# A decoder trunk on one core: the bias table's roundings, GpSimd's queue and the ninth weight chunk planned anew

## The chip, the core and the metric

The kernel runs on one core of one Trainium2 chip. A core has five engines that run beside each other, each with its own queue of instructions in a fixed order: TensorE (PE, matmuls; its weight loads are PEld), VectorE (DVE), ScalarE (ACT), GpSimd (POOL) and SyncE (SP, which here only issues transfers). Transfers between HBM and the on-chip memory run on 16 DMA engines. The metric is the device time of one execution in microseconds; lower is better. Times are compared by the median of several runs.

## What is computed

A trunk of two layers over x of 256 tokens by 1024 columns, all in float32. Layer 0 mixes tokens with a gated spatial unit, layer 1 with attention that has a relative-position bias; each layer then has a gated feed-forward part with a causal convolution of width 3. Each sub-layer ends in `x <- LayerNorm(alpha * x + f(x))`. Cut to what matters here:

```python
def conv_ffn(x, w_up, conv_w, conv_b, w_down):
    S = x.shape[1]
    h = x @ w_up                                   # (256, 1024) @ (1024, 5632)
    hp = jnp.pad(h, ((0, 0), (CONV_WIDTH - 1, 0), (0, 0)))
    hc = conv_b
    for j in range(CONV_WIDTH):
        hc = hc + conv_w[j] * hp[:, j:j + S]
    g, val = jnp.split(hc, 2, axis=-1)
    return (jax.nn.gelu(g) * val) @ w_down         # (256, 2816) @ (2816, 1024)

# in the attention: a table of 32 buckets by 16 heads, looked up by distance
s_own = s_own + bias_hb[:, rel_bucket(d_own)][None].astype(jnp.float32)
```

## The kernel before

**Two parts for each number.** TensorE multiplies in a rounded float32 format. So every weight and every activation is split into a high part (the number rounded) and a low part (what the rounding lost), and a product is three matmuls: high by high, high by low, low by high. `split` does that: ScalarE writes the rounded high part (`act`, line 381), VectorE subtracts it from the number (`tt`, line 387).

**Weights in chunks.** `stream` lists the weights in the order of their use in chunks of 128 partitions by 2048 columns, 1 MB each: among others 22 of `f_up0` (layer 0's up projection), 11 of `f_dn0` (its down projection), and the same for layer 1 (`f_up1`, `f_dn1`). A chunk of `f_dn` holds two k-steps, 128 rows of the weight each; chunk c holds k = 2c and 2c + 1. A chunk is loaded into a `raw` tile by SyncE (`load`), and `prep` has its parts written to a slot of `whi` and one of `wlo`; there are five such slots, so `spent(name, c)`, called when a chunk was used, prepares the chunk five places later. Two `raw` tiles take turns (some chunks have tiles of their own), so a load waits until the tile's last readers are done.

**Two ways to the low part.** Usually VectorE subtracts. For the chunks in `NEGATED` (from `ADDED`) and in `SIDE`, `lows` does it without VectorE's subtraction: ScalarE writes the negative of the high part into `wlo`, and a transfer that GpSimd issues reads the chunk from HBM a second time and adds it there. `ADDED` names chunk 13 of both `f_up` and chunks 1, 3 and 8 of both `f_dn`; `SIDE` is the second half of chunks 4, 5, 6 (`f_dn0`) or 5, 6, 7 (`f_dn1`). Chunks in `WHOLE`, `NEGATED` among them, are handled as one piece of 2048 columns, others in two halves of 1024. In `f_dn1` the last three chunks are in `SUMMED` too, and so in `WHOLE`: `with_sums` makes, on ScalarE, copies of some of their columns in `xt` with a row sum beside them, for the last LayerNorm.

**The down projection.** `project_out` runs over k = 0 to 15 for both token tiles t; then the last six k-steps (`TAIL`, chunks 8, 9 and 10) run for one token tile after the other, piece by piece of 512 columns. The chunks of `SEVEN` (4, 5, 6 or 5, 6, 7) are not multiplied step by step but in seven products of sums and differences (`seven`); `weight_sums` (VectorE and ScalarE) and `token_sums` (additions on GpSimd, line 634) make their operands, and `into_rest` adds their results to x on ScalarE and VectorE. `close` is the last LayerNorm.

**The bias table.** `build_bias` is called between the feed-forward part's up and down projection of layer 0. VectorE clears a buffer, four small transfers fill it, `parts` (two VectorE operations, lines 758 and 760) rounds it and writes the lost part of the table's rows, one matmul (line 772) makes the table of 16 heads by 384 distances, VectorE copies it out (line 774), and a transfer stores it (`rbscr`) for the attention, which reads it eight times.

**The order.** Nothing runs as it is recorded. `plan.op` records each operation with its engine, an estimated duration, and what it reads and writes. `Plan.emit` first gives each operation a due time, counted back from TensorE's line of matmuls; an operation's own `early` makes it due sooner. Then it plays the whole kernel through with one clock for each engine: the engine that can start first takes, of the operations that are ready, the one due first. TensorE's main matmuls keep their recorded order; those marked as fill (the table's matmul, transposes, scores) are put in when they are ready. The start times of this play give each engine's order; an operation with `after` is held until that one has been issued. On the chip each engine then runs its queue in that order, and waits at its head where an operand isn't there. In this play GpSimd's compute operations are engine "pool" and its adding transfers a separate engine "gq", with a model of a shared bus; on the chip both are one queue. `parts` is recorded as a TensorE fill of 645 ns.

## Time and profile before

| what | us |
|---|---|
| median of 3 runs | 559.65 |
| the three runs | 557.83 to 560.56 |
| the profiled execution | 558.85 |
| its span, first to last instruction | 557.1 |
| TensorE busy in it | 548.8 |
| VectorE busy | 479.1 |
| ScalarE busy | 396.5 |
| GpSimd busy | 51.7 |

A row of the timeline has start, length, engine, line, operation, the tiles written and read, shapes and a count; in brackets stands how long the engine was idle before it, and what ended the idle time. Starts are from the span's begin. The line of a helper (369, 381, 387, 391, 405) stands for many operations, so rows are told apart by tile, shape and time. Ends of matmuls are modelled: the distance from one start to the next says more than the length.

```profile
L381 ACT ACTIVATE whi<-raw 128x1024 fp32r<-128x1024 f32 (+2 forms) x150 | 175.4, 1203 | 43.4 <-DMA raw<-in_f_up 18.2
L387 DVE TENSOR_TENSOR wlo<-raw,whi 128x1024 fp32r<-128x1024 f32 (+2 forms) x138 | 186.1, 1370 | 18.1 <-ACT whi L381 16.5
...
wlo<-in_f_dn POOLq DMA_DIRECT2D x6, 1024.0 KB, 9.1
...
wlo<-in_f_dn POOLq DMA_DIRECT2D x6, 512.0 KB, 7.2
wlo<-in_f_up POOLq DMA_DIRECT2D x2, 1024.0 KB, 11.0
```

The first two rows are groups of instructions: count, busy time in all, mean length in ns, idle time before them. The others are transfers by what they write and read: count, size, and the median time from issue to landing. The six of 1 MB into `wlo` from `f_dn` are chunks 1, 3 and 8 of the two layers.

### The profile page before, as it was taken

The page shows a single profiled execution, that of the slowest core. Times are in us where ns is not written, and L with a number is a line of the kernel's source. Part 1 is how long each engine was busy: PE and PEld are TensorE (multiplying, and loading weights), DVE is VectorE, ACT ScalarE, POOL GpSimd, SP SyncE. Part 2 cuts the span into 40 slices and gives each one's busy share as a digit, 9 for nine tenths or more (in the row PEclk, how much of TensorE's full clock was granted, in tenths as well). Part 3 has the DMA queues.
Part 4 walks back from the last instruction along what each step waited for, and adds up shares of the span by engine and source line. Part 5 has one row for each costly group of instructions (what it writes and reads, how often), then busy time and mean ns, then how long its engine had stood idle before and what let it go on. Part 6 is the DMA issues. An engine that isn't in the chain of part 4 may idle for free.

```text
span 557.1 us, 8253 instructions
## 1 busy us (share of the span) xinstructions
PE 548.8 (99%) x3024; PEld 471.0 (85%) x3024; DVE 479.1 (86%) x860; ACT 396.5 (71%) x669; POOL 51.7 (9%) x60
## 2 busy tenths in 40 slices
PE   9999999999999999999999999999999999999995
PEld 6889888988898887888888888788888888888884
DVE  6699989999989888898957778798969889997687
ACT  6647576688878786845567868577747969897951
POOL 0011110000003521001000000000000000053101
PEclk9999999999999999999999999999999999999998
DMA  8979624645954799893656252725754956799832
GB/s 325 390 284 355 222 99 161 260 184 228 240 213 166 232 283 301 219 356 115 235 218 194 103 191 86 296 77 191 263 188 191 259 203 235 282 268 321 185 100 77
DMA packets 22610, 122.51 MB, mean 220 GB/s; under 512 B 2519, under 2 KB 5801, under 8 KB 10409
## 3 DMA queue, kind: packets, MB, share of 16 engines
q1 hardware_dynamic: 19240, 110.18, 53.4%
q0 software_dynamic: 3040, 11.54, 11.3%
q8 instruction: 24, 0.39, 0.3%
q10 hardware_dynamic: 288, 0.26, 0.1%
q14 instruction: 18, 0.14, 0.1%
HBM read 120.90 MB, written 1.07 MB: 219 GB/s over the span
## 4 chain that ended last, share of the span: by engine, by line
PE 63%; DVE 14%; DMA 12%; ACT 7%; issue 3%; DVEq 0%; SPq 0%; ACTq 0%
PE bank L369 40%; PE twos L369 22%; DVE wlo L387 5%; DMA raw<-in_f_up 5%; DMA raw<-in_f_dn 4%; DVE ff L391 3%; ACT whi L381 3%; DVE ff L387 2%; DMA ff<-in_f_dn 2%; DMA wlo<-in_f_dn 2%; ACT wlo L381 1%; ACT ff L381 1%; DVE x L391 1%; PE twos L375 1%; DVE rr L387 1%
## 5 line engine op out<-in xcount | busy, mean ns | idle before, releaser
L381 ACT ACTIVATE whi<-raw 128x1024 fp32r<-128x1024 f32 (+2 forms) x150 | 175.4, 1203 | 43.4 <-DMA raw<-in_f_up 18.2
L387 DVE TENSOR_TENSOR wlo<-raw,whi 128x1024 fp32r<-128x1024 f32 (+2 forms) x138 | 186.1, 1370 | 18.1 <-ACT whi L381 16.5
L369 PE MATMUL bank<-xt,whi 128*128 128x512 f32 x512 | 121.2, 391 | 0.0
L369 PE MATMUL bank<-whi,rr 128*128 128x512 f32 x354 | 112.5, 391 | 0.0
L369 PEld LDWEIGHTS bank<-xt,whi 128*128 128x128 f32 x512 | 94.7, 188 | 18.7
L369 PEld LDWEIGHTS bank<-whi,rr 128*128 128x128 f32 x354 | 66.5, 188 | 14.0 <-issue 0.3
L369 PE MATMUL twos<-xt,whi 128*128 128x512 f32 x326 | 76.3, 390 | 0.0
L369 PEld LDWEIGHTS twos<-xt,whi 128*128 128x128 f32 x326 | 60.6, 188 | 12.2
L391 DVE SCALAR_TENSOR_TENSOR ff<-ff,convc 128x255 f32<-128x255 f32 (+1 forms) x160 | 69.4, 488 | 0.5
L369 PE MATMUL bank<-wlo,rr 128*128 128x512 f32 x177 | 69.1, 390 | 0.0
L369 PEld LDWEIGHTS bank<-xt,wlo 128*128 128x128 f32 x512 | 64.2, 191 | 2.0 <-issue 0.3
L369 PE MATMUL bank<-xt,wlo 128*128 128x256 f32 x512 | 65.6, 284 | 0.0
L381 ACT ACTIVATE ff<-ff,convc 128x256 f32<-128x256 f32 x80 | 44.5, 593 | 12.2 <-DVE ff L387 12.1
L369 PE MATMUL twos<-whi,xt 128*128 128x512 f32 x128 | 42.1, 396 | 0.0
L369 PE MATMUL twos<-xt,wlo 128*128 128x256 f32 (+1 forms) x323 | 41.2, 284 | 0.0
L369 PEld LDWEIGHTS twos<-xt,wlo 128*128 128x128 f32 x323 | 40.3, 191 | 1.0
L369 PEld LDWEIGHTS bank<-wlo,rr 128*128 128x128 f32 x177 | 33.2, 188 | 6.9 <-DMA wlo<-in_f_dn 0.3
L381 ACT ACTIVATE ff<-bank 128x256 f32<-128x256 f32 (+2 forms) x62 | 23.2, 393 | 17.4 <-PE bank L369 16.4
L381 ACT ACTIVATE ff<-bank,lncol 128x128 f32<-128x128 f32 x48 | 18.9, 458 | 21.0 <-PE bank L375 21.0
L369 PEld LDWEIGHTS twos<-whi,xt 128*128 128x128 f32 x128 | 24.1, 188 | 4.7
L634 POOL TENSOR_TENSOR lnrow<-lnrow 128x128 f32<-128x128 f32 x24 | 22.6, 1130 | 45.5 <-ACT ff L381 37.5
L381 ACT ACTIVATE ff<-twos 128x512 f32<-128x512 f32 (+1 forms) x36 | 18.6, 549 | 9.2 <-PE twos L369 5.7
(158 smaller groups left out, 689.9 us busy)
## 6 DMA issues: line engine op xcount, KB each, us to landing
raw<-in_f_up SPq DMA_DIRECT2D x44, 1024.0 KB, 4.8
raw<-in_f_dn SPq DMA_DIRECT2D x20, 1024.0 KB, 6.3
raw<-in_b_qk SPq DMA_DIRECT2D x8, 1024.0 KB, 4.8
wlo<-in_f_dn POOLq DMA_DIRECT2D x6, 1024.0 KB, 9.1
lnrow<-in_lnrow SPq DMA_DIRECT2D x5, 1024.0 KB, 6.8
raw<-in_a_out SPq DMA_DIRECT2D x4, 1024.0 KB, 7.5
raw<-in_b_v SPq DMA_DIRECT2D x4, 1024.0 KB, 5.0
raw<-in_b_o SPq DMA_DIRECT2D x4, 1024.0 KB, 4.8
```

The lines of the kernel that those rows point to most:

```text
L369: nc.tensor.matmul(o, l, x, start=start, stop=stop)
L375: nc.tensor.transpose(o, x, ident.ap)
L381: return plan.op("act", ns, lambda: nc.scalar.activation(o, x, func, **kw), r, w, table=table)
L387: return dve(70 + 1.04 * flat(x), lambda: nc.vector.tensor_tensor(o, x, y, op=op), r, w)
L391: lambda: nc.vector.scalar_tensor_tensor(o, x, s, y, op0=op0, op1=op1), r, w)
L634: plan.op("pool", 1200, lambda: nc.gpsimd.tensor_tensor(o, x, y, op=op), r, w)
```

## The change

Three things, in the program alone; no product is changed.

- The ninth chunk (c = 8) of `f_dn0` and `f_dn1` leaves `ADDED`: its low part comes from VectorE's subtraction. In `f_dn1` it stays in `WHOLE`; in `f_dn0` it leaves that too and is split in two halves.
- In the plan, "gq" is gone: an adding transfer is an operation of "pool" that carries bytes. It holds GpSimd for 1200 ns, its landing is counted on a queue of all adding transfers at 170 bytes per ns with 2500 ns on top, and its own duration for the due times is 3700 + 3.0 ns per column instead of 3600 + 1.8.
- `parts` is recorded as an operation of VectorE of 500 ns that reads `raw` and writes a buffer of its own, which the table's matmul (170 ns) reads. The copy of the table's row is due 10 us sooner (`early`), and the matmul is held behind the step k = 5 of the second token tile, not k = 3.

```diff
-ADDED = {"f_up0": {13: "act"}, "f_up1": {13: "act"}, "f_dn0": {1: "act", 3: "act", 8: "act"}, "f_dn1": {1: "act", 3: "act", 8: "act"}}
+ADDED = {"f_up0": {13: "act"}, "f_up1": {13: "act"}, "f_dn0": {1: "act", 3: "act"}, "f_dn1": {1: "act", 3: "act"}}
...
-    LATE = {"pe": 200.0, "act": 140.0, "dve": 130.0, "pool": 200.0, "sp": 910.0, "gq": 910.0}
+    LATE = {"pe": 200.0, "act": 140.0, "dve": 130.0, "pool": 200.0, "sp": 910.0}
...
-        engines = ("pe", "act", "dve", "pool", "sp", "gq")
+        engines = ("pe", "act", "dve", "pool", "sp")
...
-        bus, table = 0.0, None
+        bus, added, table = 0.0, 0.0, None
...
-            if e == "gq":
+            if e == "pool" and o.nbytes:
                 bus = max(bus, s + 1100.0) + o.nbytes / 360.0
                 free[e] = s + 1200.0
-                o.end = max(bus + 1000.0, s + 2000.0 + o.nbytes / 200.0)
+                added = max(added, s + 1200.0) + o.nbytes / 170.0
+                o.end = added + 2500.0
...
     def lag(self, d, o):
+        if d.eng == "pool" and d.nbytes:
+            return 910.0
         if d.eng == o.eng:
-            return 0.0 if d.eng == "pe" else 910.0 if d.eng in ("sp", "gq") else 130.0
+            return 0.0 if d.eng == "pe" else 910.0 if d.eng == "sp" else 130.0
...
-        plan.op("gq", 3600 + 1.8 * flat(lv), lambda: nc.gpsimd.dma_start(
+        plan.op("pool", 3700 + 3.0 * flat(lv), lambda: nc.gpsimd.dma_start(
...
         b = half()
-        plan.op("pe", 645, parts, [raw], [b], True)
-        state["table"] = plan.op("pe", 1, lambda: nc.tensor.matmul(
-            b.ap[:HEADS, :DIST], cast[:two, :HEADS], cast[:two, HEADS:], start=True, stop=True), [raw], [b], True)
-        dve(400, lambda: nc.vector.tensor_copy(row.ap[:HEADS], b.ap[:HEADS, :DIST]), [b], [row])
+        c = Buf(cast)
+        dve(500, parts, [raw], [c])
+        state["table"] = plan.op("pe", 170, lambda: nc.tensor.matmul(
+            b.ap[:HEADS, :DIST], cast[:two, :HEADS], cast[:two, HEADS:], start=True, stop=True), [c], [b], True)
+        dve(400, lambda: nc.vector.tensor_copy(row.ap[:HEADS], b.ap[:HEADS, :DIST]), [b], [row]).early = 2 * SOON
...
-            if name == "f_dn0" and (k, t) == (3, NT - 1):
+            if name == "f_dn0" and (k, t) == (5, NT - 1):
                 state["table"].after = groups[-1]
```

## The prediction

> **What bounds the kernel now.** I read the page first (busy time, the row of slices, the chain), then who waited for whom, then the stretches that the change touches.

> ```profile
> span 557.1 us, 8253 instructions
> PE 548.8 (99%) x3024; PEld 471.0 (85%) x3024; DVE 479.1 (86%) x860; ACT 396.5 (71%) x669; POOL 51.7 (9%) x60
> ...
> PE   9999999999999999999999999999999999999995
> ```
> ```profile
> PE twos L772 <- DVE cast L760: 0.5, 1, 0.5
> ```
> ```profile
> 200.00:212.00 12.00, 11.54 (x54) 9.34 (x53) 10.19 (x20) 9.98 (x14) 2.10 (x2) 1.00 1.02 299
> ...
> 224.00:237.00 13.00, 13.00 (x58) 10.51 (x58) 10.10 (x10) 10.94 (x10) 1.20 (x1) 1.00 0.82 228
> 520.00:537.00 17.00, 17.00 (x76) 14.05 (x75) 11.13 (x12) 14.32 (x28) 1.22 (x1) 1.00 0.75 199
> 537.00:548.00 11.00, 11.00 (x58) 9.44 (x58) 10.73 (x20) 2.55 (x3) 1.00 (x1) 1.00 0.09 28
> 548.00:557.00 9.00, 2.38 (x20) 2.18 (x19) 5.33 (x17) 1.90 (x6) 0.91 (x1) 0.77 0.25 84
> ```

> TensorE is busy in every slice but the last, and 8.3 us of the span are not its own: the head before the first weights, some 6.7 us behind its last matmul, and one hole of half a microsecond, the table's matmul on line 772. In the stretches (columns: length, then busy time of PE, PEld, DVE, ACT, POOL, then clock, DMA share and GB/s) TensorE fills each one that the change touches except 200 to 212. So neither VectorE nor the transfers bound the kernel; they matter only where something comes late for TensorE. The change alters none of the 3024 matmuls but the place of one. It can win what TensorE waits inside the body, and a little of the tail; it can lose whatever new wait it makes.

> **The change, step by step. (a) The table's roundings.** Before, the two roundings of `parts` are recorded as TensorE work but run on VectorE; the matmul that reads them stands behind the fourth step of `f_dn0`.

> ```profile
> 211.00 0.39 PE L369 MATMUL bank<-whi,rr 128*128 128x512 f32 x1
> 211.85 0.34 PE L772 MATMUL twos<-cast 97*16 97x384 f32 x1 [0.46 <-DVE cast L760]
> 212.02 0.40 PE L369 MATMUL bank<-whi,rr 128*128 128x512 f32 x1
> ```
> ```profile
> 211.13 0.36 DVE L758 CAST cast<-ff 97x400 fp32r<-97x400 f32 x1
> 211.53 0.17 DVE L760 TENSOR_TENSOR cast<-ff,cast 33x16 fp32r<-33x16 f32 x1
> ```
> ```profile
> 228.14 0.39 PE L369 MATMUL twos<-whi,rr 128*128 128x512 f32 x1
> 228.37 0.39 PE L369 MATMUL bank<-whi,rr 128*128 128x512 f32 x1
> 228.66 0.50 PE L369 MATMUL bank<-wlo,rr 128*128 128x512 f32 x1
> 228.99 0.40 PE L369 MATMUL bank<-whi,rr 128*128 128x512 f32 x1
> ```

> ```profile
> 203.89 2.29 DVE L387 TENSOR_TENSOR wlo<-raw,whi 128x2048 fp32r<-128x2048 f32 x1 [1.48 <-ACT whi L381]
> ```

> Wide matmuls follow each other every 0.23 us (228.14 to 228.37). From 211.00 to the table's matmul it is 0.85, so 0.62 us is lost. The roundings came last: 0.36 + 0.17 us, ended at 211.70. Now the matmul stands two k-steps later (k = 5 instead of 3). A k-step is two token tiles by two pieces by three matmuls, 12 x 0.227 = 2.7 us, so it comes at about 216.7 and the roundings have 5 us more. Its own 0.17 us (211.85 to 212.02) stays. The roundings now carry a due time of their own that is long past, so VectorE will take them as soon as the plan thinks the table landed. If the plan thinks so too early, VectorE's queue stands still in front of them; the chunk that TensorE wants next (k = 4, at about 211.5) had its low part done at 206.2 (203.89 + 2.29), so some 5 us of such a halt are covered. The copy of the table's row needs its bank back before the products open, four k-steps behind 212.02, at 222.9, some 5 us after its new place. Gain between -0.6 (a halt as long as the old hole, at the new place) and +0.62; I take **0.6**, since both neighbours show 5 us of room.

> **(b) One queue for GpSimd.**

> ```profile
> 219.32 1.07 ACT L381 ACTIVATE whi<-ff 128x1024 fp32r<-128x1024 f32 x1 [1.19 <-DMA ff<-in_f_dn]
> ```

> No instruction is added. What changes is the plan: an adding transfer now counts 9.8 us instead of 7.3 for a whole chunk (3700 + 3.0 x 2048 against 3600 + 1.8 x 2048) and 6.8 instead of 5.4 for a half, so ScalarE's negations and the loads under them become due 2.6 or 1.3 us sooner. ScalarE has 2 us free in 200 to 212 to take that. The one place where such a transfer is late now is 228.37 to 228.99: two steps of 0.29 and 0.33 instead of 0.23, 0.16 us in all. Its transfer could not be planned much sooner, as ScalarE had waited for its source chunk until 219.32. Bounds: a gain of 0.16 up to a loss of one VectorE subtraction, 2.4 us (rival 3); I take **0**, the side that the row is nearer to.

> **(c) The ninth chunk.** Before, ScalarE writes the high part, then its negative, and GpSimd's transfer adds the chunk from HBM. After, VectorE subtracts.

> ```profile
> 228.35 1.90 ACT L381 ACTIVATE wlo<-whi 128x2048 fp32r<-128x2048 f32 x1
> ```
> ```profile
> 230.69 1.20 POOL L495 DMA_DIRECT2D wlo<-in_f_dn  x1 [8.04 <-ACT wlo L381]
> ```
> ```profile
> DMA to landing us min/median/max: 12.2/12.2/12.2
> ```
> ```profile
> 243.07 0.40 PE L369 MATMUL bank<-wlo,rr 128*128 128x512 f32 x1
> ```
> ```profile
> 233.59 2.36 DVE L387 TENSOR_TENSOR wlo<-raw,whi 128x1024 fp32r<-128x1024 f32 x2
> ...
> 525.79 2.29 DVE L387 TENSOR_TENSOR wlo<-raw,whi 128x2048 fp32r<-128x2048 f32 x1 [1.11 <-ACT whi L381]
> ```

> Each layer loses a 1.90 us pass of ScalarE and a 1 MB transfer, and VectorE gains 2.36 us (in `f_dn0`, where the chunk now goes in halves) or 2.29 us (in `f_dn1`, whole). VectorE is idle 2.9 us in 224 to 237 and 5.9 us in 520 to 537, so both fit, the first barely. In `f_dn0` the added part landed at 242.9 (230.69 + 12.2), and the first matmul that reads it starts at 243.07: nothing is lost there, 0.2 us from being lost. So removing it gains 0 in layer 0. In layer 1 it lies on the chain that ended last:

> ```profile
> 523.26 8.38 DMA wlo<-in_f_dn
> 531.66 2.85 ACT xt L381 x11
> 534.52 0.49 ACT ff L381
> ...
> 535.03 0.69 DVE ff L387
> ...
> 550.87 0.34 DVE x L387
> ```
> ```profile
> 550.11 0.28 PE L369 MATMUL twos<-whi,rr 128*128 128x256 f32 x1
> ```

> The copies of the sums (`with_sums`) waited for the transfer, and behind them on ScalarE stood the first copy of `into_rest` (534.52), although the products that it reads were done when the last one began, at 532.98 (row in d). With pass and transfer gone that copy can come up to 1.5 us sooner, and VectorE's run from 535.03 on with it; VectorE is full from 537 to 548 (10.73 of 11). But the end moves by little: the last addition (550.87) needs TensorE's last matmul, started at 550.11 and done some 0.3 later. So 0.4 us at most, none at least; I take **0.3**.

> **(d) The raw tile.** The ninth chunk's tile was free when ScalarE had read it; now VectorE reads it too, and the eleventh chunk's load waits for that.

> ```profile
> 520.10 0.33 SPq L405 DMA_DIRECT2D raw<-in_f_dn  x1
> ```
> ```profile
> DMA to landing us min/median/max: 5.7/5.7/5.7
> ```
> ```profile
> 532.98 0.39 PE L369 MATMUL bank<-whi,rr 128*128 128x512 f32 x1
> ```

> If the subtraction ends at X, the load lands at X + 5.7, ScalarE's pass takes 1.9 and VectorE's 2.3, so the low part is there at X + 9.9. The last product ends at 533.7 (532.98 and two more matmuls), then five k-steps of one piece come; the eleventh chunk is the fifth, 4 x 0.68 later at 536.4, its low part at 536.6. So X may be as late as 526.7; the earliest is 520.1 + 2.3 = 522.4.

> ```profile
> 521.05 1.22 DVE L387 TENSOR_TENSOR rr<-ff,rr 128x1024 fp32r<-128x1024 f32 x1 [1.36 <-ACT rr L381]
> 523.99 0.69 DVE L387 TENSOR_TENSOR rr<-lnrow,rr 128x512 fp32r<-128x512 f32 x1 [1.71 <-ACT rr L381]
> ```

> VectorE stood idle for 1.36, 1.71 and 1.11 us in front of 521.05, 523.99 and 525.79, waiting for ScalarE each time, so I take X near 524 and a cost of **0**; behind the next subtraction it would be 3.7 us (rival 2). In `f_dn0` the same load has 4 us more room.

> **The sum:** 0.6 + 0 + 0.3 = 0.9 us. The profiled execution took 558.85 us (span 557.1 and 1.75 around it), so 557.95 after. The three runs shown have their median at 559.65, 0.8 above it; I forecast **558.7** for the median, -0.2%.

> **Rivals.** About 0.5%, 2.8 us, is what a measurement of this kernel can tell from no change; the three runs alone lie 2.7 us apart.

> *1. Nothing comes out.* The hole at 211 is refilled by a wait of like size, and the tail hangs on TensorE's last matmul. For it: TensorE is 99% busy and 550.11 to 550.87 leaves little. Against: the 5 us of room. Time 559.6.

> *2. Slower: the raw tile comes free late.* VectorE takes the ninth chunk's subtraction behind the tenth's (525.79 + 2.29 = 528.1), so X = 530.4, the low part comes at 540.3 instead of 536.6, and TensorE stands for 3.7 us; behind the roundings that follow as well, which the timeline shows to end at 530.4, it is X = 532.7 and 6.0 us. It decides from X = 526.7 on. For it: VectorE's order goes by due times that come from TensorE's line, and the tile's release is a step that only lengthens a load's wait. Against: the gaps before 525.8. Time 562.4 to 564.7, say 563.

> *3. GpSimd is held.*

> ```profile
> L634 POOL TENSOR_TENSOR lnrow<-lnrow x24: 450/763/3036, 176.3 to 513.4; 128x128 f32<-128x128 f32 x24
> ```
> ```profile
> 176.78 2.39 POOL L634 TENSOR_TENSOR lnrow<-lnrow 128x128 f32<-128x128 f32 x1
> ```
> ```profile
> 176.43 2.43 DVE L387 TENSOR_TENSOR wlo<-raw,whi 128x2048 fp32r<-128x2048 f32 x1 [0.32 <-issue]
> ```

> A GpSimd addition takes 0.45 us at best and 2.39 when it starts under a VectorE subtraction of 2.43. If the joint order now puts additions ahead of a transfer that TensorE waits for already (228.66), or beside a new subtraction, that transfer is late by up to 2.4 us: 558.7 + 2.4 = 561.1. Against: the last addition of `f_dn0` was done by 196.6, and in `f_dn1` they end at 514, before the ninth chunk is there. [...]

> *4. Faster than can be seen.* All waits that the change touches come to 0.62 + 0.16 + 0.4 = 1.2 us, so only a draw of the runs gets below 556.9.

> **How the numbers follow.** Forecast 0.65; rival 1 0.17; rival 2 0.10; rival 3 0.03; rival 4 0.05. Slower by over 0.5% holds rival 2 and a sliver of the rest, 0.11; faster 0.05; within 0.5% 0.84. The range takes in the forecast with the spread of the runs (about 1.5 us either way), rival 1 and rival 3: 557.0 to 561.6. What lies outside is rival 2 and rival 4.

> **What would show it.** Right: no wait on line 772; TensorE busy 548 to 549 of some 556; four adding transfers of `f_dn` of 1 MB instead of six; the eleventh chunk's load near 524 in `f_dn1`; the first copy of `into_rest` before 534. Wrong: any wait of TensorE above 0.3 us behind 200; an `f_dn1` load of the eleventh chunk after 526.7; a GpSimd addition next to a late transfer; VectorE idle in front of the table's rounding, followed by a late chunk.

## The result, and the profile after

| | before | after |
|---|---|---|
| median | 558.96 us (10 runs, 557.52 to 562.79) | 562.92 us (10 runs, 561.01 to 564.41) |
| the profiled execution | 558.85 | 562.79 |
| its span | 557.1 | 561.1 |

The ratio is 1.0069, with a 95% interval of 1.0046 to 1.0092: 0.7% slower. The forecast was 558.7, a difference too small to tell from none, with a range of 557.0 to 561.6; the median lies 1.3 us above that range. A few numbers of the page of the changed kernel answer to those shown of before (the lines of the helpers are three higher now: 372 for matmuls, 384 for ScalarE, 390 for VectorE, 408 for loads, 498 for adding transfers, 637 for GpSimd's additions):

```profile
span 561.1 us, 8260 instructions
...
PE   9999999999999997999999999999999999999995
...
PEclk9999999999999998999999999999999999999999
...
wlo<-in_f_dn POOLq DMA_DIRECT2D x4, 1024.0 KB, 12.7
```

TensorE is no longer full in the 16th slice (each is 14 us; this one runs from 210 to 224), and the granted clock drops there too (8 tenths in that slice, 9 or more in all others). Four adding transfers of 1 MB are left of six, as planned, but their median time from issue to landing went from 9.1 us to 12.7. The view of who waited for whom has a line that was not there before:

```profile
PE bank L372 <- DMA wlo<-in_f_dn: 3.2, 1, 3.2
```

The timeline of TensorE at that place:

```profile
216.15 0.34 PE L776 MATMUL twos<-cast 97*16 97x384 f32 x1
216.32 0.40 PE L372 MATMUL bank<-whi,rr 128*128 128x512 f32 x1
219.95 0.50 PE L372 MATMUL bank<-wlo,rr 128*128 128x512 f32 x1 [3.23 <-DMA wlo<-in_f_dn]
...
221.02 0.63 PE L372 MATMUL bank<-wlo,rr 128*128 128x512 f32 x1
221.45 1.05 PE L372 MATMUL bank<-whi,rr 128*128 128x512 f32 x2
```

The table's matmul (216.15) is where the prediction put it (216.7) and waits for nothing. The second matmul behind it reads the low part of chunk 3, which isn't there: from 216.32 to 219.95 are 3.63 us instead of 0.23. After that a step takes 0.427 us (221.02 to 221.45) instead of 0.227. The windows around it show why (length, busy time of PE, PEld, DVE, ACT, POOL, then clock, DMA share, GB/s):

```profile
216.00:220.00 4.00, 0.78 (x5) 0.26 (x3) 2.26 (x4) 1.50 (x2) 0.00 (x0) 1.00 1.02 309
220.00:223.50 3.50, 3.50 (x9) 2.75 (x10) 3.47 (x5) 3.04 (x5) 1.78 (x2) 0.56 1.05 276
```

Behind the wait the granted clock is 0.56 for 3.5 us. Seven matmuls with 0.2 us too much each, and three at the edges with 0.1, make 1.7 us. So the balance up to TensorE's last matmul is 3.4 + 1.7 for the wait and the clock, less 0.62 for the table's hole and 0.17 for the two short steps at 228, which are gone: +4.3. The last matmul starts 4.4 us later than before (554.51 against 550.11), the span ends 4.0 later; the tail gave back 0.4. One late transfer is thus the whole loss of this execution.

**Why it is late.** GpSimd's queue in the changed kernel:

```profile
191.57 1.24 POOL L498 DMA_DIRECT2D wlo<-in_f_dn  x1 [52.29 <-ACT wlo L384]
...
205.56 1.22 POOL L498 DMA_DIRECT2D wlo<-in_f_dn  x1 [7.49 <-ACT wlo L384]
...
207.96 1.46 POOL L498 DMA_DIRECT2D wlo<-in_f_dn  x1
```

And before:

```profile
191.13 1.24 POOL L495 DMA_DIRECT2D wlo<-in_f_dn  x1 [2.90 <-ACT wlo L381]
...
201.36 1.22 POOL L495 DMA_DIRECT2D wlo<-in_f_dn  x1 [4.83 <-ACT wlo L381]
```

The first row of each is chunk 1's transfer of `f_dn0`, the second chunk 3's, the third (207.96) half of chunk 4. Chunk 3's is issued 4.2 us later than before. The row says that GpSimd waited for ScalarE, but ScalarE's negation of chunk 3 was even earlier than before; here is that pass after:

```profile
198.53 1.91 ACT L384 ACTIVATE wlo<-whi 128x2048 fp32r<-128x2048 f32 x1
```

and before:

```profile
199.09 1.91 ACT L381 ACTIVATE wlo<-whi 128x2048 fp32r<-128x2048 f32 x1
```

It ends at 200.44 against 201.00. The pass that the row names, a `wlo` pass of ScalarE that ends at 205.1, is chunk 4's. What did end right before 205.56 is chunk 1's transfer. The rows of the transfers of the tile `wlo` between 190 and 206 say how long they took; after:

```profile
DMA to landing us min/median/max: 13.7/14.0/14.3
```

and before:

```profile
DMA to landing us min/median/max: 8.9/9.1/9.3
```

Chunk 1's landed at 191.57 + 13.7 = 205.3 (before at 200.0), chunk 3's at 205.56 + 14.3 = 219.9 (before at 210.7), and TensorE wants it at 216.5. So there are two steps: chunk 1's transfer takes 13.7 us instead of 8.9, and chunk 3's is issued only when it has landed.

For the first step, look at the loads. In the changed kernel SyncE issues two of them, into the tiles that chunks 0 and 1 left, just ahead of chunk 1's transfer (191.57):

```profile
188.66 0.33 SPq L408 DMA_DIRECT2D raw<-in_f_dn  x1
...
189.08 0.38 SPq L408 DMA_DIRECT2D raw<-in_f_dn  x1
```

Before, one came 5.4 us ahead of the transfer (191.13), which took 4.8 us and so had landed, and the next two 3.9 us and more behind it:

```profile
185.78 0.33 SPq L405 DMA_DIRECT2D raw<-in_f_dn  x1
...
195.05 0.33 SPq L405 DMA_DIRECT2D raw<-in_f_dn  x1
...
195.47 0.83 SPq L405 DMA_DIRECT2D raw<-in_f_dn  x1
```

SyncE's order explains the shift: before, chunk 1 was loaded ahead of chunk 0 (TensorE's step k = 0 needs chunk 0 first, but chunk 1 has the longer way through GpSimd); after, chunk 0 goes first. Chunk 1's tile is free later by that, and the next load, which waits for it, slides from 5.4 to 2.9 us ahead of the adding transfer.

**Theory T:** an adding transfer with loads issued at about the same time beside it takes 5 us longer (13.7 against 8.9 here), and the space that the program sets for GpSimd's transfers (`dynamic_dma_scratch_size=1024`, line 1506 of the kernel after; called descriptor space here) doesn't hold two whole-chunk adding transfers, so that the second is held until the first has landed. The rivals: the new order of GpSimd's queue holds it by itself (R1); the ninth chunk's subtraction on VectorE does it, or the change's parts each cost something of their own, so that a cure in one place moves the trouble on (R2); nothing holds it, and only its source or its negation is late (R3).

### The profile page after: what moved, and what is told of

The parts are those of the page before. It is cut to its first block, busy times and chain, and to the rows that moved or that the text cites. A ratio compares the mean times of both kernels' runs of the same rounds, so it can differ in the third digit from the quotient of the medians.

```text
span 561.1 us, 8260 instructions
## 1 busy us (share of the span) xinstructions
PE 550.5 (98%) x3024; PEld 471.5 (84%) x3024; DVE 485.0 (86%) x863; ACT 394.5 (70%) x668; POOL 46.6 (8%) x58
## 3 DMA queue, kind: packets, MB, share of 16 engines
q0 software_dynamic: 2496, 9.44, 8.8%
HBM read 118.80 MB, written 1.07 MB: 214 GB/s over the span
## 4 chain that ended last, share of the span: by engine, by line
PE 93%; DMA 3%; DVE 2%; ACT 1%; issue 0%; DVEq 0%; ACTq 0%
PE bank L372 56%; PE twos L372 34%; DMA wlo<-in_f_dn 3%; PE twos L378 1%; PE bank L378 1%; DVE x L394 1%; DMA ff<-in_head 1%; ACT whi L384 1%; ACT wlo L384 0%; DVE ff L394 0%; ACT ff L384 0%; DVE stat L792 0%; DVE stat L832 0%; DVE whi L415 0%; DVE ff L835 0%
## 5 line engine op out<-in xcount | busy, mean ns | idle before, releaser
L390 DVE TENSOR_TENSOR wlo<-raw,whi 128x1024 fp32r<-128x1024 f32 (+2 forms) x141 | 190.7, 1371 | 17.1 <-ACT whi L384 16.7
L372 PE MATMUL bank<-whi,rr 128*128 128x512 f32 x354 | 114.3, 395 | 0.0
L372 PEld LDWEIGHTS twos<-xt,whi 128*128 128x128 f32 x326 | 60.6, 188 | 12.2
L390 DVE TENSOR_TENSOR ff<-twos,ff 128x512 f32<-128x512 f32 (+2 forms) x34 | 21.8, 652 | 5.4 <-ACT ff L384 3.5
## 6 DMA issues: line engine op xcount, KB each, us to landing
wlo<-in_f_dn POOLq DMA_DIRECT2D x4, 1024.0 KB, 12.7
```

The costliest lines, as they stand in the source:

```text
L372: nc.tensor.matmul(o, l, x, start=start, stop=stop)
L390: return dve(70 + 1.04 * flat(x), lambda: nc.vector.tensor_tensor(o, x, y, op=op), r, w)
```

## The experiments

Each ratio is to the kernel before on the same chip. Where only parts of the change are applied, they are called a (the table's roundings), b (GpSimd's queue in the plan) and c (the ninth chunk), as in the prediction.

### Twice the descriptor space, in the changed kernel

With the larger space goes a second edit: the tile of the table's roundings is laid into `xt`, which nothing else uses at that time. The control, e2, has that edit alone.

```diff
-        cast = sb.tile([P, n], F32R, name="cast")
+        cast = xt[:, :n]
...
-    nc = bacc.Bacc("TRN2", target_bir_lowering=False, num_devices=1, dynamic_dma_scratch_size=1024)
+    nc = bacc.Bacc("TRN2", target_bir_lowering=False, num_devices=1, dynamic_dma_scratch_size=2048)
```

> The changed kernel with twice the descriptor space for GpSimd's transfers (2048 bytes a partition; the table's rounded tile lies in xt to make room). Theory T: in layer 0 the adding transfer of chunk 3 could be issued only when that of chunk 1 had landed, as the space does not hold two whole chunks; with room for both it is issued by 201.5 us (ScalarE's negation ends at 200.4), lands by 213, TensorE's wait of 3.2 us for it is gone, and the time is 558.0 to 559.5. Rival R1 (the profile's own reading: GpSimd waited for ScalarE, that ended at 205.15): the issue stays at 205 to 206 and the time at 562 to 564.

> The changed kernel with the table's rounded tile in xt but the descriptor space as it was: the control of the run before. T and R1 alike: as the changed kernel, issue of chunk 3's adding transfer at 205 to 206, TensorE waits 3 us for it, 562 to 564.

With 2048 bytes: 558.85 us, ratio 1.000 (0.9987 to 1.0014), span 556.3. With 1024: 564.03 us, 1.0069 (1.0045 to 1.0093), span 560.9. Each engine's instructions stand in the same order in both. GpSimd's queue with 2048 bytes:

```profile
191.54 1.21 POOL L498 DMA_DIRECT2D wlo<-in_f_dn  x1 [52.24 <-ACT wlo L384]
...
200.76 1.21 POOL L498 DMA_DIRECT2D wlo<-in_f_dn  x1 [2.66 <-ACT wlo L384]
```

The time from issue to landing of the first of the two:

```profile
DMA to landing us min/median/max: 14.1/14.1/14.1
```

And with 1024 bytes:

```profile
205.83 1.22 POOL L498 DMA_DIRECT2D wlo<-in_f_dn  x1 [7.96 <-ACT ff L384]
```

Chunk 1's transfer is as slow as ever (14.1 us, landing at 205.6), but chunk 3's is issued at 200.76, while the first is in flight, and lands 9.8 us later at 210.6. TensorE has no wait at 216, as its window shows, and the 0.7% is gone:

```profile
216.00:220.00 4.00, 4.00 (x19) 3.27 (x18) 2.38 (x4) 3.97 (x5) 0.89 (x1) 1.00 0.80 338
```

With 1024 bytes the issue is back at 205.83, right behind the first landing (205.57). The second half of T is shown for this pair of transfers: the space holds the second one, not the order of the queue (R1), as the issue at 205.83 with 1024 bytes and at 200.76 with 2048 says. Without this accident the change is level with the kernel before. The span is 0.8 us shorter (556.3 against 557.1), but the execution that was profiled (557.97 us) is the fastest of its ten, whose median is 558.85, so this is no measured gain.

### The parts, alone and in pairs

The diffs are those of the change, cut to the part that is named.

> The change without the ninth chunk's part (it stays with the adding transfer). T: the ninth chunk has no share in the wait at 216 us, which stays: 562 to 564. Rival R2 (VectorE's two new subtractions crowd out what the wait hangs on): the wait goes and the time is 558.5 to 560.

> The change without the joint queue in the plan (the adding transfers stay an engine of their own there, with their old estimate). T: the two loads that stood just ahead of chunk 1's adding transfer came there by the new due times; without them the transfer lands near 200, chunk 3's is issued near 201, no wait at 216: 558 to 560. If the bias table's part alone orders the loads that way, 562 to 564.

> The kernel before with the joint queue in the plan alone. The loads stand in the order of the kernel before (chunk 1 of f_dn0 ahead of chunk 0). T: so chunk 1's adding transfer lands at 200 to 201, chunk 3's is issued by 201.5, and there is no wait at 216; another place may be late, as the order of VectorE and ScalarE is new: 558 to 562. If the queue alone makes the wait at 216, 562 to 564.

> The kernel before with the ninth chunk's part alone; the order of the engines hardly differs. T and my sum: TensorE still waits 0.6 us for the table's roundings, the tail is 0 to 0.4 us shorter: 558.3 to 559.2. My rival 2 (raw tile free late): the load of the eleventh chunk in f_dn1 after 526.7 and 562 or more.

> The kernel before with the table's part of the change alone (roundings as VectorE's operations, the matmul held behind k = 5). The prediction's step: no wait on the table's matmul, 0.6 us gained, nothing else: 558.2 to 558.6 beside the kernel before, ratio 0.997 to 1.0. If this part moves the loads behind 205 by itself, as it did together with the ninth chunk (R2): a wait of 1 to 3 us at 227 to 229 for chunk 5's adding transfer, and a ratio of 1.001 to 1.005.

| parts | median, us | ratio (95%) | span | TensorE's waits above 0.5 us that before has not |
|---|---|---|---|---|
| a | 568.07 | 1.0154 (1.0116 to 1.0191) | 565.7 | 1.0 at 227, 0.6 at 347, 1.2 at 449, 3.1 at 501 |
| b | 566.74 | 1.0125 (1.0083 to 1.0167) | 565.7 | 1.9 at the table's matmul, 0.7 at 229, 0.6 at 348, 0.7 at 378, 2.1 at 530 |
| c | 558.75 | 0.9988 (0.9967 to 1.0008) | 556.3 | none |
| a + b | 567.46 | 1.0139 (1.0118 to 1.0161) | 566.4 | 2.8 at 216, 3.5 at 449 |
| a + c | 561.09 | 1.0027 (1.0004 to 1.005) | 561.7 | 2.8 at 227 |
| a + b + c | 562.92 | 1.0069 (1.0046 to 1.0092) | 561.1 | 3.2 at 216 |

This fits no sum of parts. The wait at 216 comes only where a and b are together; c has no share in it, and the table's part alone, from which 0.6 us was expected, costs 1.5%. Of these expectations only that for c alone held in full. In a + b the wait at 216 stayed, as T said, but a second one took the time above 564; with a + c and with b alone it was absent, as T said, but other waits took the times above 560 and 562. The profiled execution of a + c (563.38 us) is well above its median, and the fastest took 558.51, so its wait need not be in each execution.

Every version goes through the same play of the whole kernel. With c alone nearly the old order comes out of it: its adding transfers are issued within a microsecond of those before. In all the others some adding transfer comes late for TensorE by 1 to 3.5 us. That isn't all of their loss: in a alone 1.8 us and in b alone 3.2 us of the waits listed are for other engines. In a + c the late transfer is half of chunk 5: its source chunk was third of three loads within 3.5 us, and GpSimd issues the transfer at 224.47 instead of 221.79. In a + b there is a second one, chunk 13 of `f_up1`, issued at 441.24 (before at 435.02), 2.1 and 1.7 us behind two loads, and 11.4 us from issue to landing. And a alone repeats, in the second layer, the accident that the whole change has in the first; GpSimd's queue there:

```profile
489.12 1.22 POOL L495 DMA_DIRECT2D wlo<-in_f_dn  x1 [2.17 <-ACT wlo L381]
...
504.31 1.23 POOL L495 DMA_DIRECT2D wlo<-in_f_dn  x1 [13.35 <-ACT ff L381]
```

ScalarE's pass for the second of these:

```profile
495.18 1.92 ACT L381 ACTIVATE wlo<-whi 128x2048 fp32r<-128x2048 f32 x1
```

The landing time of the first:

```profile
DMA to landing us min/median/max: 14.8/14.8/14.8
```

And TensorE's clock behind the wait:

```profile
504.00:509.70 5.70, 5.69 (x13) 4.47 (x14) 4.11 (x8) 3.24 (x5) 3.08 (x4) 0.50 0.98 290
```

Two loads were issued 0.7 and 3.2 us behind the first transfer; it takes 14.8 us and lands at 503.97, 3.1 us too late for TensorE:

```profile
489.79 2.84 SPq L405 DMA_DIRECT2D raw<-in_f_dn  x2
```
```profile
504.01 0.80 PE L369 MATMUL bank<-wlo,rr 128*128 128x512 f32 x1 [3.07 <-DMA wlo<-in_f_dn]
```

The second transfer's negation is done at 497.1, and it is issued at 504.31, right behind that landing: held for 7.2 us. A half-speed clock until 509.7 costs another 2.8 us. So both halves of T show here, in a program without b and c: 14.8 us instead of 8.3 (before, issued at 485.32), and an issue 0.3 us behind the landing. Of the expectations for a alone, the prediction's own step fails; R2's wait at 227 came (1.0 us), but the loss is three times its bound of 1.005.

### More loads ahead of chunk 1's transfer

If T is right, extra traffic in the kernel before should make the same accident. First one extra copy of chunk 3 to HBM, with 1024 bytes (e5) and 2048 (e6); then three copies of chunk 0 (e10, with 1024 bytes, and e11, with 2048). The edit of e10 is shown; e5 makes its one copy in the same way, behind chunk 3's load, and e6 and e11 have the two edits of the larger space besides:

```diff
             for x, y in cut if real is None else real:
                 queue.dma_start(x, y)
+            for z in extra:
+                queue.dma_start(z, src)
...
+        extra = [dram.tile([P, CH], F32, name=f"again{j}") for j in range(3)] if (name, c) == ("f_dn0", 0) else ()
```

> The kernel before, with one cost doubled: SyncE issues chunk 3's 1 MB load of f_dn0 a second time, into HBM scratch that nothing reads, right behind the first (about 186 us, 5 us ahead of chunk 1's adding transfer). T: an adding transfer that is issued while loads issued before it still run starts late and lands after 13 to 14.5 us instead of 8.9; with 1024 bytes the transfer of chunk 3 is then held until it landed, so issued at 203 to 206 instead of 201.4, and lands at 214 or later; need is at 216.5, so TensorE waits 0 to 4 us and the time is 559 to 563. R3 (the order of the loads does nothing to adding transfers): chunk 1's lands at 200, chunk 3's is issued at 201.4, 558.9.

> The same with 2048 bytes of descriptor space (and the table's rounded tile in xt). T: chunk 1's adding transfer lands as late as in the run before, but chunk 3's is issued at 201.0 to 201.8, as soon as ScalarE is done, while the first still runs; no wait at 216, time 558.0 to 559.8. R1: no difference to the run before.

> The kernel before, with three more loads of 1 MB behind the load of f_dn0's chunk 0: the same chunk copied three times to HBM, 4 MB in a row at some 400 KB per us, so that they are still under way when chunk 1's adding transfer is issued near 191. T: that transfer then takes 12 to 15 us instead of 8.9 and lands at 203 or later; chunk 3's, whose negation is done near 201, is issued only at that landing, not at 201.4, and lands at 213 to 219: TensorE waits where it lands after 216, by up to 3 us, and the time is 559 to 564. If GpSimd does not hold a transfer for the one before (R3): issue at 201.4 whatever chunk 1's does. The plain loads of chunks 2 and 3 come some 1 to 3 us later too, which may add a wait of up to 3 us near 212 (chunk 2's low part), the same in this run and in the next one.

> The same three copies with a descriptor space of 2048 bytes. T: chunk 1's adding transfer is as late as with 1024 bytes (landing at 203 or later), but chunk 3's is issued at 201 to 203, as soon as its negation is done and while the first is in flight, and lands 3 or more us sooner than with 1024 bytes. R3: the issue of chunk 3's transfer stands where it stands with 1024 bytes. The time is that of the run with 1024 bytes, less the wait at 216 if there is one there.

One copy: 558.75 us, ratio 0.9998 (0.9974 to 1.0022), and with 2048 bytes 559.83 us, 1.000 (0.9981 to 1.0019). A miss: the copy, issued at 185.47, landed at 192.4, 1.8 us after chunk 1's transfer was issued at 190.60, and that took 8.8 us, as without it. So one copy in flight at its issue did not lengthen it here. Three copies: 565.13 us, 1.0096 (1.0064 to 1.0128), and 564.57 us, 1.0078 (1.0045 to 1.0111). They are issued from 182.16 on:

```profile
182.16 1.85 SPq L407 DMA_DIRECT2D again<-in_f_dn  x3
185.57 16.82 SPq L405 DMA_DIRECT2D raw<-in_f_dn  x3
```

The last of the copies lands at 195.6 and chunk 3's load behind it at 200.0, so both are in flight when chunk 1's transfer is issued at 191.02. It takes:

```profile
DMA to landing us min/median/max: 15.8/15.8/15.8
```

15.8 us instead of 8.9, and the same 15.8 with 2048 bytes. That is the first half of T, made on purpose. The second half can't be read here: chunk 3's load came 9 us late itself, so its negation ended only at 206.9, when the first transfer landed (issue 207.22 and 207.19 in the two runs), and the difference that T expected didn't show. The largest of TensorE's waits in these two runs (4.3 and 3.9 us, for the table's roundings) is another thing: the table's small loads are issued at 206.40 instead of 200.54, because VectorE, which clears their buffer first, had stood 5.8 us waiting for ScalarE, and ScalarE 6.6 us for chunk 3's load.

### The old order of the two loads, in the changed kernel

```diff
+        if (name, c) == ("f_dn0", 1):
+            loads[i - 1].after = loads[i]
```

> The changed kernel with one line more: the load of f_dn0's chunk 0 is held until chunk 1's has been issued, which is the order of the kernel before; the descriptor space stays at 1024 bytes. If the lateness at 216 comes from loads that go ahead of chunk 1's adding transfer, and from nothing else that the change plans anew (T): that transfer lands within 10 us of its issue again, chunk 3's is issued near 201 and lands near 210, TensorE has no wait at 216, and the time is 558.0 to 559.5, ratio 0.997 to 1.001. If the new plan of GpSimd's queue holds chunk 3's transfer by itself, whatever the order of the loads (R1): issue near 205.5, a wait of about 3 us and 563, ratio 1.007. If the order only moves the trouble on (R2): no wait at 216 but one of 2 to 3 us at chunk 5 or in f_dn1, and 561 to 562.

565.62 us, ratio 1.0111 (1.0076 to 1.0147): no expectation held. Chunk 1 is loaded ahead of chunk 0 again, but the two are now issued at 180.53 and 180.91 instead of 178.88 and 181.89, ScalarE gets to chunk 1 later, and the two next loads, at 192.85 and 193.27, again lie 2.9 and 2.5 us ahead of the adding transfer. GpSimd's queue:

```profile
195.75 1.24 POOL L500 DMA_DIRECT2D wlo<-in_f_dn  x1 [56.51 <-ACT wlo L384]
...
210.08 1.22 POOL L500 DMA_DIRECT2D wlo<-in_f_dn  x1 [7.80 <-ACT rr L384]
```

And who TensorE waited for in it (us in total, times, longest):

```profile
PE bank L372 <- DMA wlo<-in_f_dn: 6.7, 2, 4.3
```

The first takes 14.1 us and lands at 209.82, 4.3 us late for TensorE; the second, negated by 203.4, is issued at 210.08 and makes a second wait. So the order of the two loads does not decide by itself, as T's expectation had put it. What goes with a long time is how near the next loads start. Nine of the whole-chunk adding transfers of `f_dn`:

| run and issue of the transfer | loads issued near it (us from its issue) | issue to landing |
|---|---|---|
| before, 191.13 | -5.4, +3.9, +4.3 | 8.9 |
| a + c, 200.77 | -6.3, -5.8, +5.2 | 9.1 |
| after, 487.40 | -5.3, -2.4, +5.0 | 8.3 |
| before, 523.26 | -3.2 | 8.4 |
| before, 230.69 | -3.2, -2.5, +5.3 | 12.2 |
| after, 191.57 | -2.9, -2.5, +3.9 | 13.7 |
| e9, 195.75 | -2.9, -2.5, +3.9 | 14.1 |
| a alone, 489.12 | -5.3, +0.7, +3.2 | 14.8 |
| three copies, 191.02 | four from -8.9 to -5.5, +3.9 | 15.8 |

Over the traces of all runs, count for each such transfer the loads and copies of 1 MB that have more than 1 us to run at its issue or start within 3.2 us behind it. With at most one the transfer took 8.2 to 10.9 us; with two or more 10.6 to 15.8, and once 8.9 (b alone, at 500.45, where both had started 6 us ahead). That the distance alone does it was not tested: no run moves only the loads. Chunk 1's transfer took 13.7 us with two loads in flight at its issue (after, 191.57) and 8.9 with none (before, 191.13); what the transfers share that makes the difference was not shown.

## Why the prediction was wrong

**The step that failed is (b), "One queue for GpSimd", which put the new plan's effect on the other queues at 0, and with it the sum.** It said "No instruction is added", bounded the part by "a gain of 0.16 up to a loss of one VectorE subtraction, 2.4 us" and took 0. The measured cost in this place is 5.1 us (3.4 wait and 1.7 clock). It looked only at the one transfer that was late before (228) and asked whether it could be planned sooner. It didn't ask what else the new due times move. They are used in one play of the whole kernel, together with those of (a): the loads of chunks 0 and 1 changed places, and that of a tile behind them came 2.9 us later. As neither (a) nor (b) alone makes this wait, the cost belongs to the joint plan, for which the sum had no term. Neither what loads beside it cost an adding transfer (13.7 us instead of 8.9) nor that with this space the second whole one was issued only behind the first one's landing (205.56 and 205.30) was in it, though the six transfers of the kernel before took 8.3 to 13.2 us; the median row (9.1) hid that, but two of them, 12.2 and 8.4, stood in the prediction. Its own sign of being wrong, a TensorE wait above 0.3 us behind 200, came at 216.7. What it priced in (b), the two short steps at 228, was won (0.17 us).

**(a) The table's roundings: right where it looked.** The matmul came at 216.15 (forecast 216.7) and waits for nothing; 0.62 us are gained there. But alone, this part costs 1.5%, through transfers that it doesn't touch. The prediction's bounds, 0.6 either way, are bounds for the place, not for the plan.

**(c) The ninth chunk: right.** Four adding transfers instead of six, and a tail shorter by 0.4 us, for 0.3 taken. In c alone the first copy of `into_rest` starts at 532.40, with the matmul that stood at 532.98 before now at 532.57: 1.6 us sooner seen from TensorE, for "up to 1.5". In the whole change it is 3.3 us sooner (535.55 against 537.39), so the rest comes from the new plan. The end still hangs on TensorE's last matmul. Alone the part has 0.9988 (0.9967 to 1.0008), which is no difference that can be told.

**(d) The raw tile: right in its cost of 0, by luck in its time.** The eleventh chunk's load is issued here, "near 524" having been forecast:

```profile
524.79 0.33 SPq L408 DMA_DIRECT2D raw<-in_f_dn  x1
```

But by then the changed kernel runs some 4.4 us behind, so seen from TensorE this is near 520.4. With 2048 bytes, where nothing is lost, the load is issued at 519.27, and in c alone at 521.78, both sooner than the 522.4 that the prediction called the earliest. There was more room than it thought.

**The last term of the sum.** The 0.8 us for the median over the profiled execution came from three runs; over ten it is 0.1 (558.96 against 558.85).

**The rivals.** Rival 3, an adding transfer late at GpSimd, has the right victim, but not the mechanism (the last addition ahead of 205.56 ended at 198.1), the place (it spoke against `f_dn0`) or the size (2.4 us). Rival 2, to which most of the chance of slower went, didn't come. What the prediction lacked is a rival for the plan as a whole: any change of a due time may bring loads and adding transfers together. Five of the six programs of the table ran slower than before in the median by 0.3 to 1.5%.

**What stays open.** How many bytes one such transfer needs is not measured: with 1024, two whole chunks were not in flight together, a whole one and a half were (205.56 and 207.96). A whole one and two halves were not: chunk 5's half, negated by 215.85, was issued at 220.22, behind chunk 3's landing (219.9) and with chunk 4's half in flight until 224.1. Moving the two loads away from the transfer without touching anything else wasn't managed; e9 was meant to do it. No version here beats the kernel before by more than can be measured: c alone (558.75) and the whole change with 2048 bytes (558.85) are level with it.

## What to carry to other kernels

Where a planner gives the order, price a change by the new order and not only by the edited lines: list, for each transfer that an engine can be late for, its neighbours in the other queues before and after. Look at the single times behind a median in the list of transfers; a spread from 8 to 14 us in one kind says that something decides between the two. And where a queue's issue stands behind a wait that its named releaser doesn't explain, look at which transfer landed just before it, and try more descriptor space: here 2048 bytes instead of 1024 brought the issue from 205.83 to 200.76.
